# A hybrid decoder layer on one core: two transposes, the samples' products and seven sums put elsewhere in the order

## The chip, the cores and the metric

The kernel runs on one core of one Trainium2 chip. The metric is the device time of one execution in microseconds. Three runs of the kernel before took 1736.45, 1736.59 and 1737.23 us, so the median is 1736.59.

## The reference

One inference step of a decoder layer for 256 new tokens of a prompt and 64 tokens of eight samples (8 each), 320 token columns in all, width 2048:

```python
def decoder_layer(x, ssm_state, ssm_conv_state, ffn_conv_state, p):
    h = rms_norm(x, p["norm_mix_pre"])
    proj = h @ p["w_in"]
    ...
    mix = jnp.concatenate([gate_out, ssm_out], axis=-1) @ p["w_out"]
    x = x + rms_norm(mix, p["norm_mix_post"])
    f, new_ffn_conv = conv_ffn(rms_norm(x, p["norm_ffn_pre"]), ffn_conv_state,
                               p["ffn_w_up"], p["ffn_conv_w"], p["ffn_conv_b"], p["ffn_w_down"])
    x = x + rms_norm(f, p["norm_ffn_post"])

def conv_ffn(h, conv_state, w_up, conv_w, conv_b, w_down):
    up = h @ w_up
    up, new_conv = causal_depthwise_conv(up, conv_state, conv_w, conv_b)
    g, u = jnp.split(up, 2, axis=-1)
    return (jax.nn.gelu(g, approximate=True) * u) @ w_down, new_conv
```

The inner width of the feed-forward part is 5632. All is float32. The change touches the feed-forward part alone, the second half of the kernel's time.

## The kernel before

**Products.** TensorE makes a float32 product as three products of halves: each weight slab is split into a rounded high part (whi, a cast on ScalarE) and the rest (wlo, a subtraction on VectorE), the tokens into h_hi and h_lo, and a block takes whi by h_hi (L135), whi by h_lo (L136), wlo by h_hi (L137) over 320 columns. A slab of 128 x 1024 feeds 24 such products and is loaded on SP's queue (L118) into one of three buffers, split by L124 (ScalarE) and L125 (VectorE).

**The feed-forward part** walks over 11 groups of 512 inner columns. In `ffn_up` a group's gate half and value half are projected (`project`, products `ps`), four banks of 128 columns at a time; each bank is taken out of PSUM by VectorE into a `pad` (L1359, L1360), convolved (`gcv`, `ucv`), put through gelu on ScalarE (L1372) and multiplied. While group g is projected, the down projection of group g - 1 runs as a background task, `down_steps(ck)` with ck = g - 1, which is advanced by one step (`yield`) after each 24 slab products.

**down_steps** multiplies by ffn_w_down. Its prompt part is a 2 x 2 scheme with seven products instead of eight (`product(h, i, ...)`, i from 1 to 7): weight blocks b11, b12, b21 and b22 of 128 x 1024 are loaded (L1541), differences of them are made on GpSimd (`less`, L1552, four instructions each), each is split by L1529 (ScalarE) and L1530 (VectorE), and each product is six TensorE instructions of 512 columns (`pm`, L1514). This is done for both halves of the output, h = 0 and h = 1. The seven results of each half are added up over the groups in fourteen tiles (`taken_in`: copied by ScalarE in the first group, L1506, added by VectorE afterwards, L1508). In the last of these groups (ck = 9, `last`) the seven sums of each half are joined (`together`, L1654, seven sums of 128 x 512 on VectorE); `together(0, ...)` is that of the half named in_mix, `together(1, ...)` that of in_fp. The last of the 11 groups is multiplied plainly by `down_plain` behind all that.

**The samples** are multiplied in `samples()`, once for each group while h = 1: 16 products `pms` (L1521) of 64 rows by 512 columns. Two of them, for the two halves of the columns of the array, stand beside each other. The profile counts each of the 16 twice.

**The rows of x1.** The output's residual x1 stands column by column in `acc`, and `to_rows(i)` turns a quarter of it by a VectorE transpose (L1322) into a tile in_turn and stores it by four DMAs on SP's queue (L1328) into x1_rows, from which the end of the kernel reads it. Quarters 2 and 3 are turned in the first group, at product 3 of h = 0. Their tiles (tag "gain", two buffers) and acc's own room are then used again: the block b11 of h = 1 is loaded into acc's room (it is called in_mix from there on), b12 and b22 into the two "gain" buffers (`load_beside`).

**The order** on each engine is set by a scheduler from priorities. `tc.high_priority(offset=...)` moves instructions ahead, `first()` is the highest, and `tc.issue_after(x)` keeps what follows behind instruction x on x's engine, without a wait of its own. An engine runs its queue strictly in that order.

Of the kernel before, what the change touches and what calls it, by code (L numbers as in the profile page):

```python
# [33 lines left out]
def hybrid_step(  # L34
# [10 lines left out]
    act, dve, pool, pe, sp = nc.scalar, nc.vector, nc.gpsimd, nc.tensor, nc.sync  # L45
# [57 lines left out]
    def first():  # L103

        return tc.high_priority(offset=200000)
# [26 lines left out]
    def accumulate(ps, w, xhi, xlo, first, last):  # L132
        whi, wlo = w
        made_so_far[0] += 3
        pe.matmul(ps, whi, xhi, start=first, stop=False)  # L135
        pe.matmul(ps, whi, xlo, start=False, stop=False)  # L136
        last_made[0] = pe.matmul(ps, wlo, xhi, start=False, stop=last).ins  # L137
        return last_made[0]
# [6 lines left out]

    bg, side, due, made_so_far, last_made, mixer = [], [], {}, [0], [None], []

# [1163 lines left out]
    with tc.tile_pool(name="fp", bufs=1) as fp:  # L1311
# [7 lines left out]
        def to_rows(i):  # L1319
# [5 lines left out]
            for q in range(4):  # L1325
                e = 512 * q + P * i
                with first() if i > 1 else nullcontext(), tc.issue_after(slab_load[-1]) if i == 3 else nullcontext():
                    sp.dma_start(x1_rows[:, e:e + P].rearrange("(s t) e -> t s e", t=32), st[32 * q:32 * q + 32].rearrange("p s k f -> p s (k f)"))  # L1328
# [195 lines left out]
        def down_steps(ck, parts):  # L1524
# [29 lines left out]

            def product(h, i, x, w):
                hi, lo = ready(raws[h][w])
                ps = misc("pm")
                prompt_products(ps, (parts.hi[x], parts.lo[x]), (hi, lo), True, True)
                taken_in(sums_of_m[halves[h]][i - 1], ps, ck == 0)

            def samples():
                ps = [misc("pms") for _ in range(2)]
                for h in range(2):
                    raw = raws[h]
                    sample_products(ps[h], parts.a_s, 0, (raw["b11"], raw["b12"]), True, False)
                    sample_products(ps[h], parts.a_s, 2, (raw["b21"], raw["b22"]), False, True)
                with tc.issue_after(lowered[0]):
# [11 lines left out]
            for h in range(2):  # L1579
                raw = raws[h]  # L1580
                last = h and ck == NG - 2
                product(h, 1, "a11", "b11")
                if h and ck == 0:
                    list(rows3)
                    load_beside("b22")
                yield
                one = fp.tile([P, 1024], F32, tag="t2" if h else "t1", name="one")
                less(h, "t1", "b12", "b11", one)
                if h:
                    samples()  # L1590
                if last:
                    together(0, *range(7))
                product(h, 2, "a12", "b21")
                yield
# [18 lines left out]
                product(h, 3, "s4", "b22")  # L1613
                if ck == 0 and h == 0:
                    rows3 = to_rows(3)
                    with tc.issue_after(lowered[0]):
                        list(to_rows(2))
                        next(rows3)
                if last:
# [5 lines left out]
                product(h, 6, "s2", "t2")  # L1625
                if h == 0:
                    if ck == 0:
                        room_for_sums(halves[1])
                    load(1, "b11", beside[0])
                    load_beside("b12")  # L1630
                    if ck:
                        load_beside("b22")
                yield
                if last:
                    together(1, 0, 2, 3, 4, ahead=200000)
                    summed[:] = taken
                product(h, 4, "a22", "t4")
                if h == 0:
                    load(1, "b21", fp.tile([P, 1024], F32, tag="t1", name="b21"))
# [292 lines left out]
```

## Time and profile before

| | |
|---|---|
| time, median of 3 | 1736.59 us |
| time of the profiled execution | 1736.57 us |
| its span, first to last instruction | 1734.9 us |
| granted clock of TensorE | 0.999 |
| TensorE busy | 1722.2 us |
| VectorE busy | 1334.2 us |
| ScalarE busy | 876.9 us |
| GpSimd busy | 664.2 us |
| DMA read and written | 285.00 and 22.32 MB |

In the profile PE is TensorE, DVE is VectorE, ACT is ScalarE, POOL is GpSimd and SP is the engine whose queue issues most DMAs. A row of a time line gives start, duration, engine, line and operation, output and input by the program's names (numbers of buffers left out), and in brackets how long the engine sat idle before it and what ended that. Operations of TensorE and VectorE overlap with the next one's start, so the step from one row's start to the next is what an operation takes of its engine, and the duration in the row is a little longer.

### The profile page before, as it was taken

How to read it: one execution, taken by the hardware profiler on the slowest of the kernel's cores; microseconds unless marked ns; L12 is line 12 of the kernel's file. 1: busy time of each engine (PE TensorE's matmuls, PEld its weight loads, DVE VectorE, ACT ScalarE, POOL GpSimd, SP SyncE). 2: the span in 40 equal slices, each digit the busy share in tenths (PEclk: the TensorE clock that was granted, in tenths of full speed). 3: DMA queues.
4: the chain of work that ended last, by engine and by line, in shares of the span. 5: the costliest groups of instructions: out<-in, count | busy, mean ns of one | idle time of the engine just before them, and what ended most of it. 6: DMA issues, size and time to landing. Idle time of an engine off the chain costs nothing.

```text
span 1734.9 us, 29915 instructions
## 1 busy us (share of the span) xinstructions
PE 1722.2 (99%) x11223; PEld 1607.4 (93%) x11223; DVE 1334.2 (77%) x2137; ACT 876.9 (51%) x1272; POOL 664.2 (38%) x1015
## 2 busy tenths in 40 slices
PE   9999999999999999999999999999999999999997
PEld 9999999999999999999998988989898989898985
DVE  7548864657869788788987878778787878697888
ACT  6344554333656565645555545444454545454553
POOL 2432230000424323112255546464545455554643
PEclk9999999999999999999999999999999999999999
DMA  8776665556676777665765454555545454545445
GB/s 258 222 234 191 186 173 151 157 161 189 200 232 194 230 216 218 205 208 165 231 200 182 123 179 136 171 152 155 164 144 161 138 169 135 176 130 171 135 154 165
DMA packets 216273, 310.59 MB, mean 179 GB/s; under 512 B 22080, under 2 KB 118976, under 8 KB 215936
## 3 DMA queue, kind: packets, MB, share of 16 engines
q1 hardware_dynamic: 199200, 280.81, 53.4%
q10 hardware_dynamic: 11072, 15.05, 2.5%
q0 software_dynamic: 5856, 12.83, 2.5%
q8 instruction: 88, 1.44, 0.3%
q14 instruction: 57, 0.47, 0.1%
HBM read 285.00 MB, written 22.32 MB: 177 GB/s over the span
## 4 chain that ended last, share of the span: by engine, by line
PE 95%; DVE 3%; issue 1%; ACT 1%; DMA 0%; SPq 0%; DVEq 0%; ACTq 0%
PE ps L135 20%; PE ps L137 20%; PE ps L136 20%; PE pm L1514 10%; PE pd L135 4%; PE pd L137 4%; PE pd L136 4%; PE pms L1521 4%; DVE wlo L125 1%; PE y_ps L1089 1%; PE ps_v L136 1%; PE ps_v L137 1%; PE ps_v L135 1%; PE pd L1514 1%; PE yo_ps L1004 0%
## 5 line engine op out<-in xcount | busy, mean ns | idle before, releaser
L135 PE MATMUL ps<-h_hi,whi 128*128 128x320 f32 x2428 | 750.3, 309 | 0.0
L137 PE MATMUL ps<-h_hi,wlo 128*128 128x320 f32 x2428 | 748.5, 309 | 1.7 <-DVE wlo L125 1.7
L136 PE MATMUL ps<-h_lo,whi 128*128 128x320 f32 x2428 | 748.6, 308 | 0.0
L125 DVE TENSOR_TENSOR wlo<-wraw,whi 128x1024 fp32r<-128x1024 f32 (+2 forms) x394 | 486.9, 1237 | 146.9 <-ACT whi L124 144.7
L124 ACT CAST whi<-wraw 128x1024 fp32r<-128x1024 f32 (+2 forms) x393 | 405.5, 1032 | 373.0 <-PE ps L136 148.3
L135 PEld LDWEIGHTS ps<-h_hi,whi 128*128 128x128 f32 x2428 | 455.7, 188 | 10.0 <-issue 1.3
L136 PEld LDWEIGHTS ps<-h_lo,whi 128*128 128x128 f32 x2428 | 455.9, 188 | 6.3
L137 PEld LDWEIGHTS ps<-h_hi,wlo 128*128 128x128 f32 x2428 | 455.5, 188 | 2.6 <-DVE wlo L125 2.3
L135 PE MATMUL pd<-ohi,whi 128*128 128x320 f32 x448 | 138.7, 310 | 0.0
L137 PE MATMUL pd<-ohi,wlo 128*128 128x320 f32 x448 | 138.3, 309 | 0.0
L136 PE MATMUL pd<-olo,whi 128*128 128x320 f32 x448 | 138.3, 309 | 0.0
L1529 ACT CAST whi<-b 128x1024 fp32r<-128x1024 f32 x50 | 52.4, 1048 | 79.3 <-PE ps L136 59.1
L1530 DVE TENSOR_TENSOR wlo<-b,whi 128x1024 fp32r<-128x1024 f32 x50 | 64.0, 1279 | 31.5 <-ACT whi L1529 31.5
L1377 POOL COPY ptf<-pad 128x2 f32<-128x2 f32 x88 | 41.1, 467 | 118.1 <-DVE pad L1359 116.5
L135 PEld LDWEIGHTS pd<-ohi,whi 128*128 128x128 f32 x448 | 84.1, 188 | 0.6
L136 PEld LDWEIGHTS pd<-olo,whi 128*128 128x128 f32 x448 | 84.1, 188 | 0.3
L137 PEld LDWEIGHTS pd<-ohi,wlo 128*128 128x128 f32 x448 | 84.1, 188 | 0.0
L1552 POOL TENSOR_TENSOR one<-b,one 128x256 f32<-128x256 f32 x80 | 76.9, 993 | 2.1 <-DVE wlo L1530 1.9
L248 DVE TENSOR_TENSOR acc_mix<-acc_mix,pd 128x320 f32<-128x320 f32 (+1 forms) x113 | 53.7, 478 | 28.0 <-PE pd L137 27.9
L1530 DVE TENSOR_TENSOR wlo<-one,whi 128x1024 fp32r<-128x1024 f32 x40 | 55.2, 1381 | 23.1 <-ACT whi L1529 23.0
L1521 PE MATMUL pms<-b,a_s 128*64 128x512 f32 x280 | 72.2, 596 | 0.0
L1529 ACT CAST whi<-one 128x1024 fp32r<-128x1024 f32 x40 | 41.8, 1045 | 58.6 <-PE ps L136 55.8
(426 smaller groups left out, 2800.6 us busy)
## 6 DMA issues: line engine op xcount, KB each, us to landing
wraw<-in_ffn_w_up SPq DMA_DIRECT2D x176, 512.0 KB, 3.8
wraw<-in_w_in SPq DMA_DIRECT2D x132, 512.0 KB, 4.0
b<-in_ffn_w_down SPq DMA_DIRECT2D x70, 512.0 KB, 5.3
wraw<-in_w_out SPq DMA_DIRECT2D x64, 512.0 KB, 3.6
st<-in_state_ssm SPq DMA_DIRECT2D x40, 256.0 KB, 4.4
out_ssm_state_sample<-st ACTq DMA_DIRECT2D x30, 256.0 KB, 2.9
cs<-dacs_d SPq DMA_DIRECT2D x16, 320.0 KB, 5.2
in_mix<-in_ffn_w_down SPq DMA_DIRECT2D x10, 512.0 KB, 4.0
```

Of the source, the lines that this page charges most:

```text
L124: rounded[:] = [act.copy(hi, raw).ins]
L125: lowered[:] = [dve.tensor_tensor(out=lo, in0=raw, in1=hi.bitcast(F32), op=ALU.subtract).ins]
L135: pe.matmul(ps, whi, xhi, start=first, stop=False)
L136: pe.matmul(ps, whi, xlo, start=False, stop=False)
L137: last_made[0] = pe.matmul(ps, wlo, xhi, start=False, stop=last).ins
L248: added_last[:] = [dve.tensor_tensor(out=acc[:, nb, ts], in0=acc[:, nb, ts], in1=ps[:, ts], op=ALU.add).ins]
L1377: with tc.issue_after(pool.tensor_copy(ptf[:, k, :], pad[:, 256:258]).ins):
L1514: last_made[0] = pe.matmul(ps, x[xi][:, k], w[wi][:, 512 * k:512 * k + 512], start=start and k + i == 0, stop=stop and k == 1 and i == 2).ins
L1521: last_made[0] = pe.matmul(ps[64 * h:64 * h + 64], a_s[:, k0 + k], w[h][:, 512 * k:512 * k + 512], start=start and k == 0, stop=stop and k ...
L1529: rounded[:] = [act.copy(hi, raw).ins]
L1530: dve.tensor_tensor(out=lo, in0=raw, in1=hi.bitcast(F32), op=ALU.subtract)
L1552: pool.tensor_tensor(out=room[:, cs], in0=raw[x][:, cs], in1=raw[y][:, cs], op=ALU.subtract)
```

## The change

```diff
     def accumulate(ps, w, xhi, xlo, first, last):
         whi, wlo = w
         made_so_far[0] += 3
-        pe.matmul(ps, whi, xhi, start=first, stop=False)
-        pe.matmul(ps, whi, xlo, start=False, stop=False)
-        last_made[0] = pe.matmul(ps, wlo, xhi, start=False, stop=last).ins
+        with tc.issue_after(behind_visit.pop()) if behind_visit else nullcontext():
+            pe.matmul(ps, whi, xhi, start=first, stop=False)
+            pe.matmul(ps, whi, xlo, start=False, stop=False)
+            last_made[0] = pe.matmul(ps, wlo, xhi, start=False, stop=last).ins
         return last_made[0]
...
-                with first() if i > 1 else nullcontext(), tc.issue_after(slab_load[-1]) if i == 3 else nullcontext():
+                with first() if i == 2 else tc.high_priority(offset=100000) if i == 3 else nullcontext(), tc.issue_after(slab_load[-1]) if i == 3 else nullcontext():
                     sp.dma_start(x1_rows[:, e:e + P].rearrange("(s t) e -> t s e", t=32), st[32 * q:32 * q + 32].rearrange("p s k f -> p s (k f)"))
...
-            def product(h, i, x, w):
+            def product(h, i, x, w, in_turn=False):
                 hi, lo = ready(raws[h][w])
                 ps = misc("pm")
-                prompt_products(ps, (parts.hi[x], parts.lo[x]), (hi, lo), True, True)
+                prompt_products(ps, (parts.hi[x], parts.lo[x]), (hi, lo), True, True, in_turn)
+                if in_turn:
+                    behind_visit[:] = [last_made[0]] * 8
                 taken_in(sums_of_m[halves[h]][i - 1], ps, ck == 0)
...
-                    sample_products(ps[h], parts.a_s, 0, (raw["b11"], raw["b12"]), True, False)
-                    sample_products(ps[h], parts.a_s, 2, (raw["b21"], raw["b22"]), False, True)
+                    sample_products(ps[h], parts.a_s, 0, (raw["b11"], raw["b12"]), True, False, ck == 0)
+                    sample_products(ps[h], parts.a_s, 2, (raw["b21"], raw["b22"]), False, True, ck == 0)
...
                 product(h, 1, "a11", "b11")
+                yield
                 if h and ck == 0:
                     list(rows3)
                     load_beside("b22")
-                yield
                 one = fp.tile([P, 1024], F32, tag="t2" if h else "t1", name="one")
                 less(h, "t1", "b12", "b11", one)
+                if last:
+                    together(0, *range(7))
                 if h:
                     samples()
-                if last:
-                    together(0, *range(7))
-                product(h, 2, "a12", "b21")
+                product(h, 2, "a12", "b21", ck == 0 and h == 1)
                 yield
...
                 product(h, 3, "s4", "b22")
-                if ck == 0 and h == 0:
-                    rows3 = to_rows(3)
-                    with tc.issue_after(lowered[0]):
-                        list(to_rows(2))
-                        next(rows3)
...
                 product(h, 6, "s2", "t2")
-                if h == 0:
-                    if ck == 0:
-                        room_for_sums(halves[1])
+                if h == 0 and ck == 0:
+                    rows3 = to_rows(3)
+                    with tc.issue_after(lowered[0]):
+                        list(to_rows(2))
+                elif h == 0:
                     load(1, "b11", beside[0])
                     load_beside("b12")
-                    if ck:
-                        load_beside("b22")
+                    load_beside("b22")
                 yield
...
                 product(h, 4, "a22", "t4")
+                if h == 0 and ck == 0:
+                    with tc.issue_after(lowered[0]):
+                        next(rows3)
+                    room_for_sums(halves[1])
+                    load(1, "b11", beside[0])
+                    load_beside("b12")
```

The program of TensorE, VectorE, ScalarE, GpSimd and SP holds the same instructions as before, in another order. There are three parts.

**The transposes of quarters 2 and 3** are written one and two products later. VectorE, first group (ck = 0), around the banks of the gate half of group 1 (`ps_0` to `ps_3`); `wlo<-b` is the split of b22 for product 3, `wlo<-one` and `wlo<-two` those for products 6 and 4, `wlo<-wraw` are splits of slabs. Before:

```order
L1322 STREAM_TRANSPOSE in_turn<-acc_mix 128x1280
L1359 TENSOR_TENSOR pad<-ps_1_9933,r_9643 128x256
L1360 TENSOR_TENSOR pad<-ps_1_9933,r_9643 128x8x8
L1530 TENSOR_TENSOR wlo<-b_10061,whi 128x1024
L1322 STREAM_TRANSPOSE in_turn<-acc_mix 128x1280
L1359 TENSOR_TENSOR pad<-ps_2_9934,r_9643 128x256
L1360 TENSOR_TENSOR pad<-ps_2_9934,r_9643 128x8x8
L125 TENSOR_TENSOR wlo<-wraw,whi 128x1024
L1359 TENSOR_TENSOR pad<-ps_3_9935,r_9643 128x256
L1360 TENSOR_TENSOR pad<-ps_3_9935,r_9643 128x8x8
L1530 TENSOR_TENSOR wlo<-one,whi 128x1024
L125 TENSOR_TENSOR wlo<-wraw,whi 128x1024
```

And now:

```order
L1531 TENSOR_TENSOR wlo<-b_10061,whi 128x1024
L125 TENSOR_TENSOR wlo<-wraw,whi 128x1024
L1360 TENSOR_TENSOR pad<-ps_2_9934,r_9643 128x256
L1361 TENSOR_TENSOR pad<-ps_2_9934,r_9643 128x8x8
L1323 STREAM_TRANSPOSE in_turn<-acc_mix 128x1280
L1360 TENSOR_TENSOR pad<-ps_3_9935,r_9643 128x256
L1361 TENSOR_TENSOR pad<-ps_3_9935,r_9643 128x8x8
L1531 TENSOR_TENSOR wlo<-one,whi 128x1024
L125 TENSOR_TENSOR wlo<-wraw,whi 128x1024
L1323 STREAM_TRANSPOSE in_turn<-acc_mix 128x1280
L1531 TENSOR_TENSOR wlo<-two,whi 128x1024
L125 TENSOR_TENSOR wlo<-wraw,whi 128x1024
```

The split of the slab stands right behind that of b22, the first transpose between the pads of the third and the fourth bank, the second behind two more splits. On ScalarE the cast of that slab moves behind a `gcv` (L1366) and the copy of a product (L1506). On SP's queue the eight row stores stood together ahead of the loads of b12, b11 (in_mix) and b21 of h = 1; now the order is a slab, four stores, b21, b11 (in_mix), b12, four stores, two slabs, b22.

**The samples' products of the first group** are bound behind each other, and the next slab's products behind product 2. TensorE, first group, product 1 of h = 1 (`pm`) and what follows; `ps_0` and `ps_1` are banks of the value half. Before:

```order
L1514 MATMUL pm<-whi,a_hi 128x512
L1514 MATMUL pm<-whi,a_lo 128x512
L1521 MATMUL pms<-b_10057,a_s 64x512
L1514 MATMUL pm<-wlo,a_hi 128x512
L1514 MATMUL pm<-whi,a_hi 128x512
L1514 MATMUL pm<-whi,a_lo 128x512
L1514 MATMUL pm<-wlo,a_hi 128x512
L1521 MATMUL pms<-b_10059,a_s 64x512
L1521 MATMUL pms<-b_10057,a_s 64x512
L1521 MATMUL pms<-b_10059,a_s 64x512
L1521 MATMUL pms<-b_10063,a_s 64x512
L135 MATMUL ps_0_10322<-h_hi,whi 128x320
```

Here 23 more slab products follow, then the other 11 samples' products. Now, from the end of the 24 slab products:

```order
L138 MATMUL ps_3_10317<-h_hi,wlo 128x320
L1522 MATMUL pms<-b_10057,a_s 64x512
L1522 MATMUL pms<-b_10059,a_s 64x512
L1522 MATMUL pms<-b_10057,a_s 64x512
L1522 MATMUL pms<-b_10059,a_s 64x512
L1522 MATMUL pms<-b_10063,a_s 64x512
L1522 MATMUL pms<-b_10061,a_s 64x512
```

The 16 stand in one run, ten more behind these rows. Two slab products now stand inside product 1 instead.

**The joining sums of in_mix in the last group** are written ahead of `samples()`. VectorE, ck = 9, h = 1; `in_mix<-in_mix` without a second input is a joining sum, `pms` are the samples' sums, `kept<-raw` the split of a first slab of `down_plain`. Before:

```order
L1369 SCALAR_TENSOR_TENSOR gcv<-pad,prm,gcv 128x336 x3
L1530 TENSOR_TENSOR wlo<-one,whi 128x1024
L1508 TENSOR_TENSOR in_mix<-in_mix,pms 128x512
L1508 TENSOR_TENSOR in_fp<-in_fp,pms 128x512
L1654 TENSOR_TENSOR in_mix<-in_mix 128x512
L125 TENSOR_TENSOR kept<-raw,kept 128x1024
L1508 TENSOR_TENSOR in_fp<-in_fp,pm 128x512
L125 TENSOR_TENSOR wlo<-wraw,whi 128x1024
L1654 TENSOR_TENSOR in_mix<-in_mix 128x512 x3
L1530 TENSOR_TENSOR wlo<-in_mix,whi 128x1024
```

And now:

```order
L1659 TENSOR_TENSOR in_mix<-in_mix 128x512 x3
L1531 TENSOR_TENSOR wlo<-one,whi 128x1024
L1659 TENSOR_TENSOR in_mix<-in_mix 128x512
L1370 SCALAR_TENSOR_TENSOR gcv<-pad,prm,gcv 128x336
L1659 TENSOR_TENSOR in_mix<-in_mix 128x512
L1509 TENSOR_TENSOR in_mix<-in_mix,pms 128x512
L1659 TENSOR_TENSOR in_mix<-in_mix 128x512
L1370 SCALAR_TENSOR_TENSOR gcv<-pad,prm,gcv 128x336
L1659 TENSOR_TENSOR in_mix<-in_mix 128x512
L1370 SCALAR_TENSOR_TENSOR gcv<-pad,prm,gcv 128x336
L1509 TENSOR_TENSOR in_fp<-in_fp,pms 128x512
L125 TENSOR_TENSOR kept<-raw,kept 128x1024
```

All seven sums of in_mix now stand ahead of or between the samples' sums; before, they were spread over the rest of the group. The last three taps of the gate (L1369) come later, and with them the last two gelus on ScalarE and the load of its table for the square root.

More of the change, by code (lines that the diff above doesn't have):

```diff
@@ L143, in hybrid_step @@
     hT = [None, None]
-    bg, side, due, made_so_far, last_made, mixer = [], [], {}, [0], [None], []
+    bg, side, due, made_so_far, last_made, mixer, behind_visit = [], [], {}, [0], [None], [], []
     def advance(tasks, task):
```

## The prediction

> **What bounds the kernel now.** I read the busy table first, then the waits of TensorE alone, then the time lines around each of those waits, and last the samples' products of the first and the last group beside each other.
>
> ```profile
> span 1734.9 us, 29915 instructions
> PE 1722.2 (99%) x11223; PEld 1607.4 (93%) x11223; DVE 1334.2 (77%) x2137; ACT 876.9 (51%) x1272; POOL 664.2 (38%) x1015
> PE 95%; DVE 3%; issue 1%; ACT 1%; DMA 0%; SPq 0%; DVEq 0%; ACTq 0%
> ```
>
> TensorE is busy for 1722.2 of 1734.9 us and makes 95% of the chain that ended last. So an edit pays only if it removes an idle moment of TensorE, makes its own work shorter, or shortens the tail behind its last product. The first kind is nearly used up:
>
> ```profile
> PE ps L137 <- DVE wlo L125: 1.7, 2, 1.2
> ...
> PE pd L1514 <- DVE held_w L125: 0.3, 1, 0.3
> ```
>
> Columns: total us, times, longest. Leaving the start-up aside (the line left out) there are three stalls, 1.2, 0.5 and 0.3 us, each a wait for VectorE to finish a low part of a weight slab. A cost of the second kind is not in this list, since TensorE counts as busy in it: entering and leaving the samples' products, which use half the columns of the array.
>
> **The change part by part. A, the last rows turned later.** The 1.2 us stall on the time lines of TensorE, VectorE, ScalarE and GpSimd (columns: start, duration in us; in brackets the idle time before it and what ended it):
>
> ```profile
> 894.73 0.31 PE L135 MATMUL ps<-h_hi,whi 128*128 128x320 f32 x1
> 894.88 0.31 PE L136 MATMUL ps<-h_lo,whi 128*128 128x320 f32 x1
> 896.40 0.41 PE L137 MATMUL ps<-h_hi,wlo 128*128 128x320 f32 x1 [1.21 <-DVE wlo L125]
> 896.65 0.31 PE L135 MATMUL ps<-h_hi,whi 128*128 128x320 f32 x1
> ...
> 887.75 1.76 DVE L125 TENSOR_TENSOR wlo<-wraw,whi 128x1024 fp32r<-128x1024 f32 x1
> 889.43 0.41 DVE L1359 TENSOR_TENSOR pad<-ps,r 128x256 f32<-128x256 f32 x1
> 889.89 1.50 DVE L1322 STREAM_TRANSPOSE in_turn<-acc_mix 128x1280 f32<-128x1280 f32 x1
> 891.76 1.54 DVE L1530 TENSOR_TENSOR wlo<-b,whi 128x1024 fp32r<-128x1024 f32 x1
> 893.23 1.50 DVE L1322 STREAM_TRANSPOSE in_turn<-acc_mix 128x1280 f32<-128x1280 f32 x1
> 895.10 1.25 DVE L125 TENSOR_TENSOR wlo<-wraw,whi 128x1024 fp32r<-128x1024 f32 x1
> ...
> 890.01 0.67 ACT L1366 ACTIVATE gcv<-pad,prm 128x336 f32<-128x336 f32 x1 [2.33 <-DVE pad L1360]
> 890.58 1.04 ACT L1529 CAST whi<-b 128x1024 fp32r<-128x1024 f32 x1
> 891.52 1.05 ACT L124 CAST whi<-wraw 128x1024 fp32r<-128x1024 f32 x1
> 892.47 0.58 ACT L1506 COPY in_fp<-pm 128x512 f32<-128x512 f32 x1
> ...
> 890.77 3.84 POOL L1552 TENSOR_TENSOR two<-one,b 128x256 f32<-128x256 f32 x4
> ```
>
> Products of this form follow each other at 0.15 us (894.73, 894.88). The third was due at 895.03 and began at 896.40, and the next came 0.25 behind it where 0.15 is usual: the stall costs 1.37 + 0.10 = 1.47 us. The wlo it waited for began at 895.10, behind two transposes of 1.43 us each (step to the next row). Its ScalarE half was ready at 892.6, so VectorE's queue is to blame.
>
> In the changed order that wlo stands right behind the one at 891.76, and no transpose ahead of it. Now ScalarE decides: after the change it has a gcv (0.57, the step 890.01 to 890.58) and the copy (0.48) before the cast, so the cast ends at 891.52 + 0.57 + 0.48 + 1.05 = 893.62. The wlo starts at 893.65 and lasts 1.22 to 1.76 us: VectorE's splits take 1.76 (row at 887.75) where GpSimd subtracts beside them, and GpSimd is at it until 894.6. It ends at 894.87 to 895.41, and TensorE's third product starts within 0.05 us of that: the stall left is 0 to 0.43, and 0.10 with it if there is any.
>
> The transposes are not gone. The first now stands between the pads of the third and fourth bank. From the end of the wlo: pad 0.46 (889.43 to 889.89), transpose 1.43, pad 0.46, so the fourth bank is free at 897.2 to 897.7. TensorE wants it 18 products after 894.73, at 897.4. The delays don't add, since a late third product moves that date too. The second stands behind two more splits of 1.15, at 899.8; the split after it ends at 902.4. It belongs to the product two rounds on, due at 903.6 (a round is 24 products at 0.147 and six at 0.23, 4.9 us, so 894.73 + 4.9 + 3.5 + 0.46). A gains 0.9 to 1.47; bounds from outside are 0 (the transposes hold the next product as they held this one) and 1.47. I take 1.2, near the inner range's middle.
>
> [...]
>
> **B, the samples' products in one run.** First group, then last group:
>
> ```profile
> 909.56 0.39 PE L1514 MATMUL pm<-whi,a_hi 128*128 128x512 f32 x1
> 910.12 1.07 PE L1521 MATMUL pms<-b,a_s 128*64 128x512 f32 x2
> 912.25 1.94 PE L1521 MATMUL pms<-b,a_s 128*64 128x512 f32 x8
> 917.86 1.50 PE L1521 MATMUL pms<-b,a_s 128*64 128x512 f32 x5
> 919.20 0.59 PE L1521 MATMUL pms<-b,a_s 128*64 128x512 f32 x1
> 919.63 0.59 PE L1521 MATMUL pms<-b,a_s 128*64 128x512 f32 x1
> 924.65 0.31 PE L135 MATMUL ps<-h_hi,whi 128*128 128x320 f32 x1
> ...
> 1651.79 0.40 PE L1514 MATMUL pm<-whi,a_hi 128*128 128x512 f32 x1
> 1656.80 3.65 PE L1521 MATMUL pms<-b,a_s 128*64 128x512 f32 x16
> 1665.31 0.31 PE L135 MATMUL ps<-h_hi,whi 128*128 128x320 f32 x1
> ```
>
> Both stretches hold the same work: one product of six, 24 slab products, 16 samples' products (each counted twice), another product of six. The first group cuts the 16 into runs of 1, 4 and 11 and takes 924.65 - 909.56 = 15.09; the last group has them in one run and takes 1665.31 - 1651.79 = 13.52. The difference, 1.57 us, is what binding saves. It also comes out of its parts: two halves run beside each other in steps of 0.43 us (919.20, 919.63); the odd runs of 1 and 11 leave one product each without a partner (2 x 0.43), and two entries and exits less make the other 0.71. The change adds no instruction. Bounds: 1.4 to 1.6, the lower one if the slab products that now interleave with the first product lose a step.
>
> **C and D, the joining sums ahead.** The other two stalls:
>
> ```profile
> 1680.63 0.40 PE L1514 MATMUL pm<-whi,s_hi 128*128 128x512 f32 x1
> 1681.54 0.41 PE L137 MATMUL ps<-h_hi,wlo 128*128 128x320 f32 x1 [0.51 <-DVE wlo L125]
> ...
> 1663.96 0.69 DVE L1508 TENSOR_TENSOR in_fp<-in_fp,pms 128x512 f32<-128x512 f32 x1 [2.75 <-PE pms L1521]
> 1668.52 2.01 DVE L1654 TENSOR_TENSOR in_mix<-in_mix 128x512 f32<-128x512 f32 x3
> 1680.27 1.21 DVE L125 TENSOR_TENSOR wlo<-wraw,whi 128x1024 fp32r<-128x1024 f32 x1
> ...
> 1711.11 0.40 PE L1514 MATMUL pd<-held_w,a_lo 128*128 128x512 f32 x1
> 1711.79 0.74 PE L1514 MATMUL pd<-held_w,a_hi 128*128 128x512 f32 x2 [0.28 <-DVE held_w L125]
> ```
>
> Products of 512 columns follow at 0.23, so the second stall costs 1681.54 - 1680.86 = 0.68, with the slow restart 0.78; the third 1711.79 - 1711.34 = 0.45, with it 0.55. VectorE idled 2.75 us for the samples' sum at 1663.96 while seven sums of 0.67 us stood behind them. Now they fill that gap. Walking the changed order from there: the second sample sum is done at the same 1664.65; the cast of the next slab comes 2 us later on ScalarE, since the last gelu and a table load now follow the taps, but is needed only at 1670.2 (1665.31 + 24 x 0.147 + 6 x 0.23); by 1680.3 three sums less stand ahead of the wlo, of which waits for TensorE's banks and ScalarE eat most, and it starts some 0.6 us sooner, at 1679.6 to 1679.7. It ends at 1680.9. The filler at 1680.63 now comes after, so TensorE is there at 1680.63 and waits 0.3 + 0.1: C gains 0.4, between 0 and 0.78. By 1711 the last two of the seven are gone from the queue too, 1.3 us before a stall of 0.45: D gains 0.45, between 0 and 0.55.
>
> **The sum.** 1.2 + 1.57 + 0.4 + 0.45 = 3.6 us. The profiled execution took 1736.57 us for its span of 1734.9; the median of the runs shown is 1736.59, the same. The tail behind the last product stays. 1736.57 - 3.6 = **1733.0 us**, 0.21% faster. A measurement of this kernel can tell about 0.2% from no change, 3.47 us here, so the forecast lies on that line.
>
> **The rivals.** *First: the transposes take their stall along.* They must still run by the time that in_mix is loaded, in the stretch where VectorE is busy without a pause. For it: from 893.65 to 902 the changed order leaves no gap on VectorE. Against it: each later split has 0.3 us or more in hand. If A gives 0.4 or less, and C too little to count, 0.4 + 1.5 + 0.1 + 0.4 = 2.4: 1734.2 us. A milder form: the split that starts at 893.65 is held until GpSimd's last subtraction ends at 894.6 and then takes its 1.22, to 895.8; A keeps 0.5, the sum 2.9, 1733.7 us. Against it: the splits at 887.75 and 891.76 ran inside GpSimd's work and were only 0.3 to 0.5 longer.
>
> *Second, the slower side: the weights of the second half come too late.*
>
> ```profile
> 897.85 0.64 SPq L1541 DMA_DIRECT2D in_mix<-in_ffn_w_down  x1
> 904.18 2.83 POOL L1552 TENSOR_TENSOR one<-b,in_mix 128x256 f32<-128x256 f32 x4 [6.06 <-DMA in_mix<-in_ffn_w_down]
> ...
> in_mix<-in_ffn_w_down SPq DMA_DIRECT2D x10, 512.0 KB, 4.0
> ```
>
> This load goes into the room of the residual, so it must wait for both transposes; with the second done at 901.2 it is issued at 901.3, 3.4 us later, behind four row stores and one slab on SP's queue. It took 6.3 us (897.85 to 904.18) when eight stores were in front; its usual is 4.0 (the last row, the median of ten); with four in front I expect 5.0, so 906.3. Cast 1.05 and split 1.22 follow, and the third step of the half's first product is due at 909.1 (894.73 + 0.3 left of the stall + 2 rounds + 3.5 + 0.46 and two slab products): no stall until 906.8. At 6.3 us it lands at 907.6 and costs 0.8: 1733.8 us. Beyond that each us costs one, and the whole gain is gone at 901.3 + 9.1 = 910.4; no load of this stretch came near (6.3 is the one that waited longest). A 10 us landing would give 1737.5 us.
>
> [...]
>
> *Third: it does what it says, and VectorE's and ScalarE's new order in the last group does harm* (the late cast at 1668.4 slips past 1670.2). It needs 1.8 us more than walked; with 0.5 lost, C and D gone: 1734.3 us.
>
> **How the numbers follow.** Forecast 60%; its own range is 1732.2 (1.47 + 1.6 + 0.78 + 0.55 = 4.4) to 1733.9 (0.9 + 1.5 + 0.1 + 0.2 = 2.7). First rival 20% (5 of them its milder form), a late load that costs part of the gain 10%, the last group's harm 6%, slower than before 4%. The range that should hold 8 in 10 reaches over the first three rivals' times but not to a lost gain: 1732.2 to 1735.2. Faster by over 0.2% (under 1733.1) is 44%: some seven tenths of the forecast's 60 and a little of the rest. Within 0.2% is 52%. Slower by over 0.2% is 4%: the slower case needs a landing after 913.9 for that, and I leave it the rest for an order that I walked wrongly.
>
> **What would show it.** Right: TensorE's waits list loses the 1.2 us entry near 895 or keeps 0.4 or less; one row of samples' products in the first group, 13.5 us from its first product to the next slab; no wait at held_w near 1708. Wrong: a wait of TensorE on pad L1360 or on in_mix's cast near 897 or 907; a wait over 0.5 near 1678; a first group that takes over 14 us with its samples' products in one run.

## The result and the profile after

The changed kernel takes 1733.94 us (median of 22 runs, 1732.94 to 1734.86), the kernel before in the same runs 1736.61. The ratio is 0.9985, with a 95% interval of 0.998 to 0.9991: 2.67 us faster, 0.15%; the whole interval lies below 1, and the gain is smaller than the 0.2% by which the prediction told a change from none. The forecast was 1733.0. The profiled execution of the change took 1733.47 us, its span 1731.8: 3.1 us less than the span before. So one execution shows more than the median of 22, and a good part of what follows is about that difference.

The head of the page after, and behind it the waits of TensorE (total us, times, longest):

```profile
span 1731.8 us, 29920 instructions
PE 1720.6 (99%) x11223; PEld 1607.6 (93%) x11223; DVE 1336.1 (77%) x2137; ACT 876.5 (51%) x1272; POOL 671.0 (39%) x1015
```

```profile
PE early L69 <- DVE ones L65: 1.1, 1, 1.1
PE ps L138 <- DVE wlo L125: 0.5, 2, 0.3
```

(Line numbers from L135 on are one higher than before, later ones up to five.) The 1.2 us stall and the wait at held_w are gone. Two are left, 0.2 and 0.3 us; the first of them is new.

To see where the time went I compare the starts of the same product in two profiles. Two stretches hold all of it: the *first stretch*, from the first product of the first group (873.72 before, 873.76 after) to the product at 956.47 before and 954.07 after; and *the rest*, from there to the end. The two products on TensorE's time line, before and after:

```profile
873.72 0.39 PE L1514 MATMUL pm<-whi,a_hi 128*128 128x512 f32 x1
...
956.47 0.40 PE L1514 MATMUL pm<-whi,a_hi 128*128 128x512 f32 x1
```

```profile
873.76 0.39 PE L1515 MATMUL pm<-whi,a_hi 128*128 128x512 f32 x1
...
954.07 0.39 PE L1515 MATMUL pm<-whi,a_hi 128*128 128x512 f32 x1
```

| place | saved, us | predicted |
|---|---|---|
| A, the stall near 896 | 1.32 | 1.2 |
| B, first product of the second half to the next slab, 15.09 to 14.06 | 1.03 | 1.57 |
| a late split near 946, gone | 0.10 | - |
| **first stretch** | **2.45** | 2.77 |
| C, the stall near 1681 (to the product at 1698.11, now 1695.58) | 0.13 | 0.4 |
| D, held_w | 0.56 | 0.45 |
| **the rest** | **0.70** | 0.85 |

A as the time lines show it (start, duration in us, in brackets the idle time before and what ended it):

```profile
891.70 1.64 DVE L1531 TENSOR_TENSOR wlo<-b,whi 128x1024 fp32r<-128x1024 f32 x1 [1.22 <-ACT whi L1530]
893.69 1.33 DVE L125 TENSOR_TENSOR wlo<-wraw,whi 128x1024 fp32r<-128x1024 f32 x1 [0.35 <-ACT whi L124]
895.41 1.49 DVE L1323 STREAM_TRANSPOSE in_turn<-acc_mix 128x1280 f32<-128x1280 f32 x1
...
892.61 1.05 ACT L124 CAST whi<-wraw 128x1024 fp32r<-128x1024 f32 x1
...
890.83 4.80 POOL L1553 TENSOR_TENSOR two<-one,b 128x256 f32<-128x256 f32 x4
...
895.08 0.41 PE L138 MATMUL ps<-h_hi,wlo 128*128 128x320 f32 x1
```

The slab's split starts at 893.69, four hundredths from the walk, right after its cast. It runs inside GpSimd's subtractions (890.83 to 895.63) and ends at 895.02, and TensorE's third product starts at 895.08, its turn; a slow restart of 0.1 is what remains of 1.47 (a product at 897.53 is 0.04 late besides). No later split is held by the transposes.

B: the 16 samples' products are one run now, but something else has come in:

```profile
908.76 0.37 PE L136 MATMUL ps<-h_hi,whi 128*128 128x320 f32 x1
908.97 0.31 PE L137 MATMUL ps<-h_lo,whi 128*128 128x320 f32 x1
...
910.70 0.42 PE L138 MATMUL ps<-h_hi,wlo 128*128 128x320 f32 x1 [0.20 <-DVE wlo L125]
...
906.66 1.05 ACT L1530 CAST whi<-in_mix 128x1024 fp32r<-128x1024 f32 x1 [1.10 <-DMA in_mix<-in_ffn_w_down]
907.61 1.05 ACT L124 CAST whi<-wraw 128x1024 fp32r<-128x1024 f32 x1
...
907.74 1.23 DVE L1531 TENSOR_TENSOR wlo<-in_mix,whi 128x1024 fp32r<-128x1024 f32 x1 [4.04 <-ACT whi L1530]
908.88 1.76 DVE L125 TENSOR_TENSOR wlo<-wraw,whi 128x1024 fp32r<-128x1024 f32 x1
...
901.06 0.39 SPq L1542 DMA_DIRECT2D in_mix<-in_ffn_w_down  x1
...
908.15 5.73 POOL L1553 TENSOR_TENSOR one<-b,in_mix 128x256 f32<-128x256 f32 x4 [8.48 <-DMA b<-in_ffn_w_down]
```

in_mix is issued at 901.06 and lands at 906.6, 5.5 us later. ScalarE idles 1.10 us for it and VectorE 4.04, with the next slab's cast and split queued behind. in_mix's own product is in time. But the slab's split starts only at 908.88 and takes 1.76, and TensorE's third product of that slab starts 0.36 after its due time, with 0.11 behind it and 0.06 ahead: 0.53 of B's 1.57.

### The profile page after: what moved, and what is told of

Same layout as the page of the kernel before. It is cut to its first block, busy times and chain, and to the rows that moved or that the text cites. A ratio compares the mean times of both kernels' runs of the same rounds, so it can differ in the third digit from the quotient of the medians.

```text
span 1731.8 us, 29920 instructions
## 1 busy us (share of the span) xinstructions
PE 1720.6 (99%) x11223; PEld 1607.6 (93%) x11223; DVE 1336.1 (77%) x2137; ACT 876.5 (51%) x1272; POOL 671.0 (39%) x1015
## 4 chain that ended last, share of the span: by engine, by line
PE 98%; DVE 1%; DMA 0%; ACT 0%; issue 0%; POOL 0%; DVEq 0%; ACTq 0%
PE ps L136 20%; PE ps L138 20%; PE ps L137 20%; PE pm L1515 11%; PE pd L136 4%; PE pd L138 4%; PE pd L137 4%; PE pms L1522 4%; PE pd L1515 1%; PE y_ps L1090 1%; PE ps_v L136 1%; PE ps_v L138 1%; PE ps_v L137 1%; PE yo_ps L1005 0%; PE up_ps L1022 0%; PE pds L1522 0%
## 5 line engine op out<-in xcount | busy, mean ns | idle before, releaser
L1016 POOL TENSOR_TENSOR st<-st,tote 128x512 f32<-128x512 f32 x32 | 47.0, 1499 | 61.2 <-DMA st<-in_state_ssm 38.4
```

Source lines behind the costliest of these rows:

```text
L1016: pool.tensor_tensor(out=by_head(st[h]), in0=by_head(st[h]), in1=tote[:, h0:h0 + 8, 4 * h + i:4 * h + i + 1].to_broadcast([P, 8, 64]), op= ...
```

## The experiments

Three questions: is the wait at 910.70 the price of the moved transposes, of the binding, or of both; what makes in_mix late; and why does the median show less than the profile? Every kernel is compared by its two stretches.

**The parts one by one.** `no_binding` drops the second part, `no_move` the first:

```diff
# no_binding
-                    sample_products(ps[h], parts.a_s, 0, (raw["b11"], raw["b12"]), True, False, ck == 0)
+                    sample_products(ps[h], parts.a_s, 0, (raw["b11"], raw["b12"]), True, False)
...
-                product(h, 2, "a12", "b21", ck == 0 and h == 1)
+                product(h, 2, "a12", "b21")
# no_move: to_rows(2), to_rows(3) and the loads of b11 and b12 back at products 3 and 6
```

> The change without its second part: the samples' products of the first group are free again and stand in runs of 1, 12 and 3. Measure: the first stretch, from the first product of the first group (873.72 before, 873.76 with the change) to the product that starts at 956.47 before and 954.07 with the change; the change saved 2.44 us there. Theory: the 0.20 us wait at 910.70 with its late restart (0.47 in all) and the 0.06 ahead of it need both parts at once, the late load of in_mix (first part) and the slab's products that the binding pulls forward (second part). So this kernel loses the 1.57 that binding is worth and gets 0.53 back: no wait of TensorE on a slab's split near 911, 1.4 us saved in the first stretch, time 1735.0. Rival: the late load alone makes the wait, so it stays: 0.9 saved, time 1735.5.

> The change without its first part: both transposes stand where they stood before, the eight row stores ahead of the loads. Theory: the 1.2 us wait near 896 is back (1.42 lost with its restart), and the binding is worth its full 1.57, since in_mix is loaded at 897.9 and nothing waits near 911: 1.55 saved in the first stretch, time 1734.8. Rival: the 0.5 us is what the binding itself costs (slab products that interleave with product 1): 1.0 saved, time 1735.4. Both expect the last groups as in the change (0.7 saved behind 954.07).

`no_binding`: 1.39 saved in the first stretch, no wait near 911; 1734.60 us against 1736.51 (0.999, 0.998 to 0.9999). `no_move`: 1.55 saved, 1.2 us wait back, none near 911; 1733.98 (0.9987, 0.9978 to 0.9996). Both stretches are as the theory had them, 0.5 from the rivals; both medians are lower than expected (1735.0 and 1734.8). So the binding is worth its 1.57 where in_mix is early, and a late load (5.4 us in the profile of `no_binding`) costs nothing where the slab's products aren't pulled forward. Together they cost 0.53. The rest is the change's in both (0.60 and 0.67 saved). One thing does not fit the profiles: by its median `no_move` is as fast as the whole change (1733.98 and 1733.94). Moving the transposes, worth 0.9 us in the profiles, is worth nothing in the median. (The profile of `no_move` is of an execution of 1734.75, the top of its ten runs.)

**GpSimd beside the split, and a later load.**

```diff
# less_later
+                if h and ck == 0:
+                    seen = pool.tensor_copy(fp.tile([P, 4], F32, name="seen"), low_part[0][:, 0:4].bitcast(F32)).ins
+                    with tc.issue_after(seen):
+                        less(h, "t1", "b12", "b11", one)
# in_mix_late
+                    list(rows3)
-                    load(1, "b11", beside[0])
+                    load(1, "b11", beside[0], stored[0])
```

> The change, but GpSimd's subtraction b12 - b11 of the first group starts behind the split of b21 (a tiny copy of that split's result, 128 x 4, is added on GpSimd ahead of it); all other engines keep their order. Theory: GpSimd's work beside the slab's split at 908.88 made it 1.76 us long where splits alone take 1.22, and that 0.54 is more than the wait: the split ends at 910.1, TensorE's third product of the slab is due at 910.35, the wait is gone, and the first stretch saves 2.9 instead of 2.44 (time 1733.4). Rival: it is the load alone, the split keeps its length: 2.44 saved, wait of 0.2 stays (time 1733.9).

> The change, but the four stores of the second transpose and the load of b12 stand ahead of the load of in_mix on SP's queue: issue at 904.7 instead of 901.06. Theory (the prediction's second rival, doubled): in_mix then lands near 910.0 instead of 906.6, its product waits for its cast until 911.1 (due at 908.3), then again about 0.7 for its split, then about 0.3 to 0.5 for the slab's: 3.0 to 3.8 lost less the 0.53 already there, so that the first stretch saves -0.1 to -0.9 instead of 2.44 and the time is 1736.4 to 1737.2: the gain gone. Rival: the issue order matters less than the crowd of transfers, in_mix lands 4 us behind its issue, at 908.7: 1.3 to 2.0 lost, time 1735.2 to 1735.9.

`less_later`, VectorE, GpSimd and ScalarE:

```profile
909.65 1.22 DVE L125 TENSOR_TENSOR wlo<-wraw,whi 128x1024 fp32r<-128x1024 f32 x1
...
912.49 3.93 POOL L1553 TENSOR_TENSOR one<-b,in_mix 128x256 f32<-128x256 f32 x4
...
907.42 1.05 ACT L1530 CAST whi<-in_mix 128x1024 fp32r<-128x1024 f32 x1 [2.62 <-DMA in_mix<-in_ffn_w_down]
```

The split takes 1.22 and the wait on it is gone, as the theory said. But the first stretch saved 1.37, not 2.9: in this execution in_mix landed 7.0 us behind its issue (900.31), where nothing ahead of it had been changed, and TensorE waited 0.8 us for its cast and 0.2 for the slab's. The theory on the split holds; the sum was wrong by the load. The median, 1733.74 (0.9983, 0.9974 to 0.9993), can't tell it from the change.

`in_mix_late` takes 1739.80 us (1.0017, 1.0008 to 1.0027) and loses 3.88 in the first stretch: worse than the theory's worst by 3.0. TensorE:

```profile
911.83 0.79 PE L1515 MATMUL pm<-whi,a_hi 128*128 128x512 f32 x1 [3.31 <-ACT whi L1530]
...
913.92 0.63 PE L1515 MATMUL pm<-whi,a_hi 128*128 128x512 f32 x1
914.35 0.63 PE L1515 MATMUL pm<-whi,a_lo 128*128 128x512 f32 x1
```

and its table by stretches (length, busy time of PE, PEld, DVE, ACT and POOL with their instructions, granted clock, DMA share, GB/s):

```profile
911.00:911.40 0.40, 0.00 (x0) 0.00 (x0) 0.00 (x0) 0.40 (x1) 0.40 (x1) 1.00 0.75 251
911.50:912.00 0.50, 0.17 (x1) 0.17 (x2) 0.19 (x1) 0.50 (x2) 0.50 (x2) 0.50 0.92 274
912.00:915.00 3.00, 2.72 (x6) 1.71 (x7) 3.00 (x3) 1.67 (x2) 3.00 (x3) 0.50 0.66 246
915.00:918.00 3.00, 3.00 (x12) 2.90 (x12) 3.00 (x3) 1.53 (x2) 0.54 (x1) 0.50 0.57 174
918.00:922.00 4.00, 4.00 (x25) 2.66 (x25) 3.80 (x8) 2.25 (x4) 1.25 (x6) 0.97 0.42 136
```

in_mix lands at 910.7, 5.8 us behind its issue at 904.88. The stall of 3.31 us is what the theory reckoned with. The granted clock falls to 0.50 at 911.4, 2.9 us into the stall, and stays there until 918.2, 6.4 us behind the start of the first product after the stall (911.83), and products follow at 0.43 and 0.27 us instead of 0.23 and 0.147. Six long and twelve short products took 6.52 us (911.83 to 918.35) where 3.16 and a wait of 0.28 were due: the slow clock cost 3.1 us, two slow restarts included. In the stretches that hold the stalls of 0.2 to 1.2 us in other profiles it reads 1.00 (893 to 898 in before and `no_move`, 909 to 911 in the change, 907 to 911 in `less_later`). How long a stall has to be to lower the clock, one case doesn't show.

**When does in_mix land, and what is in its way?** `again` is the changed kernel itself. `b21_last` changes the order of three loads. `slab_first` leaves the load late and makes TensorE need it later.

```diff
# b21_last: on SP in_mix, a store, b12, b21; in the change b21, in_mix, b12
-                    load_beside("b12")
+                    b12_load = load_beside("b12")
-                    load(1, "b21", fp.tile([P, 1024], F32, tag="t1", name="b21"))
+                    load(1, "b21", fp.tile([P, 1024], F32, tag="t1", name="b21"), b12_load if ck == 0 else None)
# slab_first: in slab(), behind the slab's cast and split
+        while behind_split:
+            behind_split.pop()()
...
+                if h and ck == 0:
+                    behind_split.append(lambda: product(1, 1, "a11", "b11"))
+                else:
                     product(h, 1, "a11", "b11")
```

> The changed kernel once more, nothing altered: a second look at when in_mix lands. In the profiles so far that load took 5.5 us (the change, no_binding) and 7.0 us (less_later) from the same place of the order, so theory: its landing differs from execution to execution, and the cost of the late load with it, from 0.5 us at 5.5 to about 1.6 at 7.0; this profile shows a landing between 5.5 and 7 us and 1.4 to 2.4 us saved in the first stretch. Rival: 5.5 is the rule and 7.0 belongs to the later subtraction: 5.5 again, 2.4 saved. Time 1733.9 either way.

> The change, but product 1 of the second half is written behind the next slab's splits: on ScalarE and VectorE the slab's cast and split (its data are there at about 900) stand ahead of in_mix's, and so do the gate's taps; on TensorE five slab products stand ahead of product 1 and eight inside it. Theory: what is late is in_mix alone, and the slab's split only stood behind it; now TensorE needs in_mix's cast at 909.0 and its split at 910.8 instead of 908.3 and 908.8, so a landing up to about 908 costs nothing: no wait near 907 to 911, 2.9 us saved in the first stretch even with a landing of 7 us, time 1733.2 or less. Rival: eight taps ahead of in_mix's split (0.5 us each beside nothing, up to 0.9 beside GpSimd) make VectorE late instead: a wait of TensorE for in_mix's split of 0.5 to 1.5 us, 1.4 to 2.4 saved, time 1734 to 1734.5.

> The change, but on SP's queue b21 is loaded behind in_mix and b12 instead of ahead of in_mix. Theory: what makes in_mix take 5.5 to 7 us is the 512 KB of b21 issued 1.3 us ahead of it, and without it the load lands 4.0 to 4.7 us behind its issue (at 905.1 to 905.8): no wait near 908 to 911, 2.9 us saved in the first stretch, time 1733.3. Rival: the crowd is that of the stores and later slabs, and the load still takes 5.5 or more: 2.4 saved or less, time 1733.9; b21 itself, issued at 902.7, could then be the next that is late (its cast is due about 918).

`again`, ScalarE and TensorE's waits:

```profile
907.54 1.04 ACT L1530 CAST whi<-in_mix 128x1024 fp32r<-128x1024 f32 x1 [2.70 <-DMA in_mix<-in_ffn_w_down]
```

```profile
PE pm L1515 <- ACT whi L1530: 0.9, 1, 0.9
PE ps L138 <- DVE wlo L125: 0.5, 2, 0.3
PE ps L136 <- ACT whi L124: 0.2, 1, 0.2
```

The same kernel: issue at 900.32, landing at 907.5, 7.1 us. Only 0.83 of the 2.45 is left in the first stretch. TensorE waits three times, for in_mix's cast, the slab's cast and the slab's split, 2.1 us with the restarts. The landing does differ from execution to execution, as the theory had it, and both ends were worse than reckoned (7.1 us against 7, 0.83 saved against 1.4). `less_later` saved 0.54 more with a landing as late: there GpSimd did not make the slab's split longer. 11 runs gave 1734.14, from 1733.06 to 1736.56, against 1736.24 before (0.9989, 0.998 to 0.9998).

`b21_last`, the issue and ScalarE, and all waits of TensorE:

```profile
900.24 0.39 SPq L1542 DMA_DIRECT2D in_mix<-in_ffn_w_down  x1
...
904.18 0.59 ACT L1507 COPY in_fp<-pm 128x512 f32<-128x512 f32 x1 [2.39 <-PE pm L1515]
904.85 1.05 ACT L1530 CAST whi<-in_mix 128x1024 fp32r<-128x1024 f32 x1
```

```profile
PE early L69 <- DVE ones L65: 1.1, 1, 1.1
PE ps L138 <- DVE wlo L125: 0.3, 1, 0.3
```

in_mix lands 4.5 us behind its issue, no wait is left between 890 and 960, and 2.97 is saved, where 2.9 was expected. 1732.29 us (0.9977, 0.9969 to 0.9986), its runs from 1731.72 to 1733.08; the time expected was 1733.3, 1.0 more. So b21, 512 KB issued 1.3 to 1.9 us ahead, was what stood in the way: with it in front in_mix took 5.4 to 7.1 us in five profiles of this order, and 4.3 to 4.5 in three without. What that is worth in an ordinary run is best read from `again`, measured beside this kernel: 1734.14 against 1732.29, 1.85 us, and ten of its eleven runs lie above the slowest of this one. The profiles lie on both sides of that: 0.52 less saved in the change's than in this one, 2.14 less in `again`'s. And against the 1.55 that `no_move` saves in the first stretch the first part is worth 1.42 here, near the 1.47 of the forecast's upper end: the late load was what hid it in the median. The packets fit. In the profile of the change the four stores issued behind in_mix (packets of 512 B) put none on the DMA engines between 901.5 and 906.0 and 23 in the half microsecond after; all that time the engines take packets of 2 KB, the loads. So these stores can hardly have delayed in_mix, which landed at 906.6; b21, issued ahead, did. (Whether b12 did, a load issued behind in_mix with packets of the same size, is not shown.)

`slab_first`: 2.76 saved, 1733.10 (0.9981, 0.9972 to 0.999), no wait for in_mix or the slab, with a landing of 6.3 us. It lost 0.24 behind 908.78, where the product that needs in_mix's cast came late by 0.14 and restarted. The eight taps did not make VectorE late. Theory right, size 0.1 off.

**A version that is faster than the change in both stretches.** In the last group, the tap and products of the value half's second bank, which nobody needs before 1691, stood ahead of the split that TensorE waits for:

```diff
# best: slab_first, b21_last and this; both_ends: b21_last and this
-                        how.enter_context(first())
+                        how.enter_context(first() if j != 1 else tc.high_priority(offset=100000))
```

> The change with both of these, and in the last group the second bank of the value half (tap, product a, a_s) put behind the slab's split that TensorE waits for at 1678.72. Theory: no wait near 896 to 911 (2.9 us saved in the first stretch), and that split starts 0.9 us sooner, at about 1676.5, so that the third stall (0.49 with 0.11 behind it) goes: 1.3 us saved behind 954.07 where the change saved 0.7; together 4.2, time 1732.5. Rivals: in_mix stays late (first stretch as in the change); or the values that now come later make the last products wait: behind 954.07 0.7 or less.

> b21_last, and in the last group the later second bank of the kernel best, without slab_first's part. Theory: slab_first's taps ahead of in_mix's split cost best 0.2 us in the first stretch (2.78 saved there against 2.98 in b21_last), and the later second bank is worth 0.61 by itself (1.30 saved behind 954.07 against 0.69): 2.98 + 1.30 = 4.3 saved, a span 0.2 shorter than best's for the same start, time 1731.8; no wait of TensorE on VectorE or ScalarE is left behind the start-up. Rival: the two parts of the first group help each other against a landing that differs from run to run, so without slab_first a wait near 908 comes back: 2.4 or less there, time 1732.3 or more.

`best` 1732.00 us (0.9976, 0.9967 to 0.9985), 2.78 and 1.30 saved. `both_ends` 1731.99 (0.9976, 0.9967 to 0.9985), 3.01 and 1.30. In `both_ends` the split starts at 1676.15 and ends at 1677.37, 0.2 ahead of the third product at 1677.58, and the start-up's is TensorE's only wait in the whole kernel:

```profile
1676.15 1.22 DVE L125 TENSOR_TENSOR wlo<-wraw,whi 128x1024 fp32r<-128x1024 f32 x1
...
1677.44 0.31 PE L137 MATMUL ps<-h_lo,whi 128*128 128x320 f32 x1
1677.58 0.31 PE L138 MATMUL ps<-h_hi,wlo 128*128 128x320 f32 x1
```

```profile
PE early L69 <- DVE ones L65: 1.1, 1, 1.1
```

The two fixes of the first group do not add; the order of the loads alone is the better one by 0.2 in the profiles. The medians of `best` and `both_ends` can't be told apart, and `best` is only 0.29 below `b21_last`, measured beside it: the 0.6 of the later second bank is seen in two profiles and not confirmed by the medians. Expected were 1732.5 and 1731.8.

| kernel | in_mix, issue to landing | first stretch saved | median, us (before beside it) |
|---|---|---|---|
| the change | 5.5 | 2.45 | 1733.94 (1736.61) |
| again (the same) | 7.1 | 0.83 | 1734.14 (1736.24) |
| no_move | 6.5, issued 2.9 earlier | 1.55 | 1733.98 (1736.51) |
| no_binding | 5.4 | 1.39 | 1734.60 (1736.51) |
| less_later | 7.0 | 1.37 | 1733.74 (1736.51) |
| in_mix_late | 5.8, issued 3.8 later | -3.88 | 1739.80 (1736.51) |
| slab_first | 6.3 | 2.76 | 1733.10 (1736.24) |
| b21_last | 4.5 | 2.97 | 1732.29 (1736.24) |
| best | 4.3 | 2.78 | 1732.00 (1736.24) |
| both_ends | 4.4 | 3.01 | 1731.99 (1736.31) |

## Why the prediction was right in its time and wrong in one step

**A was right.** VectorE's queue was the cause, the split follows ScalarE's cast at 893.69 (walked: 893.65) and no stall is left: 1.32 in the profile of the change, 1.29 in that of `b21_last`, where 1.2 from 0.9 to 1.47 was forecast. The first rival (the transposes take their stall along) did not come, and its milder form neither: a split held until GpSimd's last subtraction ends would have started at 895.6. It ended at 895.02. But the reason given against that form, that splits inside GpSimd's work had been only 0.3 to 0.5 longer, does not tell whether a split is held. GpSimd's row at 890.83 stands for four subtractions; the last three of them one by one:

```profile
891.52 0.73 POOL L1553 TENSOR_TENSOR two<-one,b 128x256 f32<-128x256 f32 x1
892.22 1.72 POOL L1553 TENSOR_TENSOR two<-one,b 128x256 f32<-128x256 f32 x1
893.91 1.72 POOL L1553 TENSOR_TENSOR two<-one,b 128x256 f32<-128x256 f32 x1
```

A subtraction that starts beside no split takes 0.73 to 0.75. The two that start beside a split take 1.72, and each ends 0.6 after that split does (893.94 after 893.34, 895.63 after 895.02). Each of the two splits in turn ends 1.1 after the subtraction that was running when it started (893.34 after 892.25, 895.02 after 893.94), about the step of a split that stands alone. So what made these splits longer goes with the one subtraction that was running at their start, not with the whole row; why it does is not shown. The prediction took the row of four for one instruction. The split at 887.75 (1.76) in the profile of before fits too: it ends at 889.51, 1.1 after a subtraction that started at 886.70 and took 1.72. The slab's split at 908.88 is another such case, 1.76, to 910.64, 1.1 after a subtraction that ends at 909.57; in `less_later`, where GpSimd starts later, it takes 1.22.

**B was right in size and lost a third of it to a step I had walked wrongly: the second rival.** Without the late load the binding saves 1.55 (`no_move`; forecast 1.57). The step that failed is "this load ... with four in front I expect 5.0, so 906.3 ... no stall until 906.8". Both halves were wrong. The landing: I counted the four stores and "one slab" in front and gave them 1.0 us over the usual 4.0; but b21 was directly in front, and the load took 5.4 to 7.1. Before, b21 was loaded behind in_mix, now ahead of it; I had this order before me and did not price it. The 6.3 us of the kernel before was misread in the same way. I put it down to eight stores, but a load stood in front there too, b12, 0.8 us ahead:

```profile
897.06 0.74 SPq L1541 DMA_DIRECT2D b<-in_ffn_w_down  x1
```

Nor was 6.3 the longest of that stretch, as the prediction has it: the loads issued at 898.59 and 905.14 took 6.7 and 7.2 us. The stall: I asked when in_mix's own product needs its split (909.1) and not what is queued behind in_mix on ScalarE and VectorE. The next slab's cast and split are, and with the binding that slab's third product is due at 910.35. The split came 0.36 late for that with in_mix at 906.6, so in_mix had to be there by about 906.25, not 906.8. The rival had 10% and 0.8 us for a 6.3 us landing; it came in all three profiles that have this order of loads, the binding, and product 1 in its place, and cost 0.5, 1.6 and 2.1 (the change, `less_later`, `again`, against the 2.97 of `b21_last`).

**Beyond the landing, the price was not one for one.** "The whole gain is gone at 910.4" and "a 10 us landing would give 1737.5" took each us for a us. At a landing of 910.7 the time was 1739.8: the stall of 3.3 us cost another 3.1 by the granted clock of 0.50.

**C was right in kind and too large: 0.13 instead of 0.4** (0.19 at the stall itself, 0.06 lost again in the products behind it). The step is "it starts some 0.6 us sooner". In before's profile and the one after:

```profile
1675.10 1.30 DVE L1530 TENSOR_TENSOR wlo<-b,whi 128x1024 fp32r<-128x1024 f32 x1
```

```profile
1672.91 1.65 DVE L1531 TENSOR_TENSOR wlo<-b,whi 128x1024 fp32r<-128x1024 f32 x1
1677.46 1.21 DVE L125 TENSOR_TENSOR wlo<-wraw,whi 128x1024 fp32r<-128x1024 f32 x1
...
1678.09 0.31 PE L137 MATMUL ps<-h_lo,whi 128*128 128x320 f32 x1
1678.72 0.42 PE L138 MATMUL ps<-h_hi,wlo 128*128 128x320 f32 x1 [0.32 <-DVE wlo L125]
```

The split that TensorE waits for moved from 1680.27 to 1677.46, 2.81 sooner, of which 2.40 had been won before: 0.41, not 0.6. The split of b ahead of it takes 1.65 instead of 1.30: GpSimd is at work beside it in both orders, and the subtraction running at its start now has 0.6 us left (to 1673.47) instead of 0.2 (to 1675.31); the split ends 1.1 after that in both (1674.56, 1676.40). And the filler product that hid 0.23 of the stall is gone, as forecast. **D was right**: no wait at held_w, 0.56 for 0.45 (the restart, 0.11, went with it). The third rival (harm by the late table load and casts) did not come; ScalarE's casts were in time.

**The sum.** A 1.32, B 1.55, C 0.13 and D 0.56 make 3.56, with the unforeseen 0.10 near 946 3.66; the forecast was 3.6: that these agree is in part luck, since errors of 0.1 to 0.3 in A, C and D cancelled. What the forecast lacks is the late load, and this differs from execution to execution: 0.5 in the profile of the change (3.1 saved), 2.1 in `again` (1.5 saved). The medians, 2.67 and 2.10 saved, lie between. The time, 0.94 above the forecast, lies just outside the forecast's own range (to 1733.9) and in the wider one, because that one held a late load.

## What to carry to other kernels

When a load is moved behind another one on its queue, price the one in front (here 512 KB, and 1 to 3 us), and ask not only when the load's own product needs it but what stands behind it in the queues of the engines that wait. Splits that stand behind one late load become late together, and a part that pulls products forward (here the binding) can turn another part's slack into a stall: walk the parts in combination. One profile of a kernel with a load near its limit is one draw: two profiles of this one differ by 1.6 us in 80.

## What the runs showed that I had not expected

The same load, at the same place of the same order, took 5.5 us in one execution and 7.1 in another; with b21 behind it, 4.5, 4.3 and 4.4 in three. Why the crowded landing differs so much was not found. The start of the first group, long before the change's work, lies between 872.72 and 874.08 in the profiles, so that times of 1 us apart can be start-up alone; stretches measured from the same product agree within 0.15 us in the rest of the kernel (777.65 to 777.79 in all profiles with the change's last groups). A stall of 3.3 us cost 6.6: 3.5 of delay and 3.1 at a granted clock of 0.50 behind it. And in the cases looked at one by one, a split of VectorE ended 1.1 us after the subtraction of GpSimd that was running when it started, and a subtraction that started beside a split ended 0.6 after that split.
